# A second feed-forward product as two nested levels of seven half-size products, in two phases around the other block's first product

## The chip, the core and the metric

The kernel runs on one core of a Trainium2 chip. The metric is the device time of one execution in microseconds. The program before takes 2951.67 us (median of three runs, 2950.88 to 2952.83). All matrices are fp32 and lie in DRAM; a matmul reads its two operands from SBUF and adds into PSUM.

## The reference

One transformer layer on 2048 tokens of width 1024. The change touches the last step, the feed-forward part with squared ReLU:

```python
def sq_relu_mlp(h, w1, w2):
    return jnp.square(jax.nn.relu(h @ w1)) @ w2
...
        h2 = modulate(x, norm2_g[l], sh2, sc2)
        x = x + g2 * sq_relu_mlp(h2, w_ff1[l], w_ff2[l])
```

`w_ff1` is 1024 x 4096, `w_ff2` is 4096 x 1024. `g2` is one factor per channel (M2 in the kernel), `x` the residual (x1_d).

## The kernel before

Everything is held transposed: 128 channels on the partitions, 512 tokens (TB) along a row. The four groups of 512 tokens form two blocks of 1024.

**Precision.** TensorE multiplies fp32r operands. Each fp32 operand is split into a high half h (a cast on ScalarE, ACT) and a low half l = x - h (a subtraction on VectorE, DVE). A product of two operands is three matmuls, hh, hl and lh (`product`, lines 1971 to 1973). Each has 128 x 128 weights and 512 moving columns.

**Seven products.** A matrix product of 2 x 2 quarters is made of seven products of quarters, with sums of quarters as operands and of results behind them (the Strassen-Winograd form). The before kernel does that at one level in both feed-forward products.

**Four stages**, in this order: `ff1(0)`, `ff2(0)`, `ff1(1)`, `ff2(1)`; the number is the block.

- `ff1` (first product) runs over 16 groups of 256 hidden channels. `ff1_group` makes seven products per group, adds the results on DVE (line 1981; five of the additions read PSUM, four read SBUF alone), applies ReLU and square on ACT, and stores the seven operands that `ff2` needs: `ao_d[blk][p]`. `w1_ops` prepares the weights of the next group beside it.
- Beside `ff1(0)`, `w2_ops` reads two row tiles of `w_ff2` per group, forms four sums on DVE (lines 1957 to 1961) and stores the seven weight operands, `wo_d[p]` (printed as w2o_d).
- `ff2` (second product) runs over seven products p and 8 chunks c each, 56 steps. A step loads 512 KB of `ao_d` and 512 KB of `wo_d`, splits both (`ff2_cast`, lines 2088 and 2089), and makes 24 matmuls into four PSUM banks. The results are added up in PSUM where possible, then scaled by M2 and added to the residual on DVE (`scaled`, line 2123), and stored.
- Beside `ff2(0)`, `h_ops` and `mod_part` prepare the operands of `ff1(1)`. GpSimd (POOL) has nothing to do in any of the four stages.

**What sets the order.** Each engine works its instructions in the order of the program, and waits by semaphores. In `ff2` that order is pinned to the code's. Loads and stores are issued by SyncE (SP), in order too. Buffers come in rings by tag (POOLS): b4 and f2 hold 1024 and 512 fp32 columns, hb 512. A load waits until the oldest buffer of its ring is free.

Of the kernel before, what the change touches and what calls it, by code (L numbers as in the profile page):

```python
# [48 lines left out]
SPLIT = (2, 0)  # L49


def f32(ap):
# [48 lines left out]
class Kern:  # L101
# [127 lines left out]
    def constants(self):  # L229
# [81 lines left out]
        self.wo_d = operands("w2o")  # L311
# [1426 lines left out]
    def halves(self, raw, p=None, kk=None):  # L1738
        nc = self.nc
        tags = ("hb", "hb")  # L1740
        if p in (0, 5):
            tags = ("in", "in")
        elif p == 1 and kk < 3:
            tags = (("raw", "raw"), ("raw", "gx"), ("gx", "hb"))[kk]
        h, l = (self.sb(t, [TB], F32R) for t in tags)
        nc.scalar.copy(h, raw)
        nc.vector.tensor_tensor(out=l, in0=raw, in1=f32(h), op=ALU.subtract)
        return h, l
# [103 lines left out]
    def h_ops(self, blk, ops, mod):  # L1852
# [3 lines left out]
        xs, r, turned = [], None, 0  # L1856

        def quarters():
            for kk in range(HK):
                x = self.sb("f8", [2, 2, TB])  # L1860
                xs.append(x)
                for i in range(2):
                    for j in range(2):
                        while kk > turned + 1:
                            yield
                        self.x1_quarter(x, blk, kk, i, j)
                        yield

        loads = quarters()
        for at, _ in enumerate(mod):  # L1870
            if at >= 3:
                next(loads, None)
            if 6 <= at < 9:
                r = next(spread)
            yield
        for kk in range(HK):
            x = xs[kk]
            self.x1_scaled(x, r)
            next(loads, None)
            yield  # L1880
            raw = self.x1_turned(x, kk)
            turned += 1
            yield
            next(loads, None)
# [6 lines left out]
            next(loads, None)  # L1891
# [4 lines left out]
            next(loads, None)  # L1896
# [48 lines left out]
    def w2_ops(self, s):  # L1945
        nc = self.nc
        tt, sub = nc.vector.tensor_tensor, ALU.subtract
        rows = self.I["w_ff2"][0]
        r = self.sb("f9", [2, 2, TB])
        nc.sync.dma_start(  # L1950
            r.rearrange("p j n c -> p j (n c)"),
            rows[2 * s * P : (2 * s + 2) * P].rearrange("(j p) c -> p j c", p=P),
        )
        yield
        b11, b12, b21, b22 = r[:, 0, 0], r[:, 0, 1], r[:, 1, 0], r[:, 1, 1]
        t1, t2, t3, t4 = (self.sb("f2", [TB]) for _ in range(4))
        tt(out=t1, in0=b12, in1=b11, op=sub)
        tt(out=t2, in0=b22, in1=t1, op=sub)
        yield
        tt(out=t3, in0=b22, in1=b12, op=sub)  # L1960
        tt(out=t4, in0=b21, in1=t2, op=sub)
        yield
        for p, src in enumerate((b11, b21, b22, t4, t1, t2, t3)):
            nc.sync.dma_start(self.wo_d[p][s // 2][s % 2], src)
        yield
# [77 lines left out]
    def ff1(self, blk, h, extra, w=None, late=()):  # L2043
        if w is None:
            w = {0: {}}
            for _ in self.w1_ops(0, w[0]):
                pass
        late = iter(late)
        for g in range(NG):
            nxt = iter(())  # L2050
            if g + 1 < NG:
                w[g + 1] = {}
                nxt = self.w1_ops(g + 1, w[g + 1])
            else:
                raws = [self.ff2_load(blk, 0, c) for c in range(2)]
                self.ready = [self.ff2_cast(raws.pop(0))], raws
            more = extra(g)
            for _ in self.ff1_group(blk, g, w.pop(g), h):
                next(late, None)
                next(nxt, None)  # L2060
                next(more, None)
            for _ in nxt:
                pass
            for _ in more:
                pass

    def ff2_load(self, blk, p, c, apart=False):
        raw = []
        for src in (self.ao_d[blk][p][c], self.wo_d[p][c]):
            if apart:  # L2070
                ls = [self.sb("hb", [TB], F32R) for _ in range(2)]
                for s, l in enumerate(ls):
                    self.nc.sync.dma_start(f32(l), src[s])
            else:
                ls = self.sb("b4", [2, TB], F32R)
                self.nc.sync.dma_start(f32(ls), src.rearrange("s p c -> p s c"))
            raw.append(ls)
        return raw

    def ff2_cast(self, raw):  # L2080
        nc = self.nc
        out = []
        for ls in raw:
            apart = isinstance(ls, list)
            pairs = []
            for l in ls if apart else [ls]:
                h = self.sb("hb", [TB], F32R) if apart else self.sb("b4", [2, TB], F32R)
                nc.scalar.copy(h, f32(l))  # L2088
                nc.vector.tensor_tensor(out=l, in0=f32(l), in1=f32(h), op=ALU.subtract)  # L2089
                pairs += [(h, l)] if apart else [(h[:, s], l[:, s]) for s in range(2)]  # L2090
            out.append(pairs)
        return out

    def ff2(self, blk, side):
        nc = self.nc
        add, mult = ALU.add, ALU.mult
        order = (0, 1, 5, 6, 4, 2, 3)
        steps = [(p, c) for p in order for c in range(NCH)]
        ahead = 4 if blk else 3

        def load(n):
            return self.ff2_load(blk, *steps[n], blk and n > 2 and n % 2)

        begin = self.here()
        ready, raws = self.ready
        raws += [load(n) for n in range(2, ahead)]
        stores = []
        goes = {1: (0, 0), 4: (1, 1), 2: (0, 1), 3: (1, 0)}
        u2, u3, xs = ([None] * TT for _ in range(3))

        def place(p, t):
            i, j = goes[p]
            return 2 * blk + i, j * TT + t

        def residual(p):
            for t in range(TT):
                b, k = place(p, t)
                xs[t] = self.sb("f2", [TB])
                nc.sync.dma_start(xs[t], self.x1_d[b][k * P : (k + 1) * P, :])

        def scaled(p, t, out, src):
            _, k = place(p, t)
            nc.vector.scalar_tensor_tensor(  # L2123
                out=out, in0=src, scalar=self.M2[:, k : k + 1], in1=xs[t], op0=mult, op1=add
            )

        def carried(p, ts):
            for t in ts:
                scaled(p, t, xs[t], (u3 if p == 4 else u2)[t])

        def leave(p, t, src):
            b, k = place(p, t)
            c = self.sb("f2", [TB])
            scaled(p, t, c, src)

            def store(queue=nc.sync):
                queue.dma_start(
                    self.out[k * P : (k + 1) * P, b * TB : (b + 1) * TB], c
                )

# [48 lines left out]
        for _ in side:  # L2189
            pass  # L2190
# [459 lines left out]
```

## Time and profile before

| | us |
|---|---|
| median of three runs | 2951.67 |
| the profiled execution | 2947.45 |
| its span on the core | 2945.7 |
| `ff1(0)`, from 1698.8 | 315.6 |
| `ff2(0)`, from 2014.4 | 311.1 |
| `ff1(1)`, from 2325.5 | 309.9 |
| `ff2(1)`, from 2635.4 | 306.2 |

The stages are bounded by where the operands of the matmuls change in the trace. The profile has one line of tenths per engine, in 40 slices of the span (a 9 is busy for 90% or more). Its groups of instructions give engine, operation, out<-in by tile name, shape and count, then busy us and the mean ns of one. PE is TensorE's matmuls, PEld its weight loads.

### The profile page before, as it was taken

How to read it: one execution, taken by the hardware profiler on the slowest of the kernel's cores; microseconds unless marked ns; L12 is line 12 of the kernel's file. 1: busy time of each engine (PE TensorE's matmuls, PEld its weight loads, DVE VectorE, ACT ScalarE, POOL GpSimd, SP SyncE). 2: the span in 40 equal slices, each digit the busy share in tenths (PEclk: the TensorE clock that was granted, in tenths of full speed). 3: DMA queues.
4: the chain of work that ended last, by engine and by line, in shares of the span. 5: the costliest groups of instructions: out<-in, count | busy, mean ns of one | idle time of the engine just before them, and what ended most of it. 6: DMA issues, size and time to landing. Idle time of an engine off the chain costs nothing.

```text
span 2945.7 us, 39124 instructions
## 1 busy us (share of the span) xinstructions
PE 2880.6 (98%) x14062; PEld 2177.6 (74%) x14062; DVE 2037.2 (69%) x2946; ACT 1393.3 (47%) x1997; POOL 674.3 (23%) x472
## 2 busy tenths in 40 slices
PE   8999999999999999999999999999999999999999
PEld 7877788777555555447888878888888888888887
DVE  6857387875888988877555797876676666654554
ACT  6545765552455554554222354444463444444442
POOL 0000000000999999983333200000000000000000
PEclk9999999999999999999999999999999999999999
DMA  8688867786110100117666578888766543456663
GB/s 312 192 297 275 300 214 232 251 268 223 51 34 30 37 31 26 34 58 248 203 212 197 170 264 300 310 288 302 255 237 232 172 148 140 148 185 247 229 219 143
DMA packets 387955, 568.04 MB, mean 193 GB/s; under 512 B 41952, under 2 KB 180880, under 8 KB 387760
## 3 DMA queue, kind: packets, MB, share of 16 engines
q1 hardware_dynamic: 375456, 544.83, 55.2%
q10 hardware_dynamic: 12304, 20.71, 1.9%
q8 instruction: 110, 1.80, 0.3%
q14 instruction: 85, 0.70, 0.1%
HBM read 382.78 MB, written 182.58 MB: 192 GB/s over the span
## 4 chain that ended last, share of the span: by engine, by line
PE 73%; DVE 3%; DMA 2%; ACT 1%; issue 1%; SPq 0%; POOL 0%; DVEq 0%; ACTq 0%; POOLq 0%
PE b L1971 13%; PE b L1973 13%; PE b L1972 13%; PE o L2534 8%; PE s L2520 7%; PE b L215 4%; PE b L217 4%; PE b L216 4%; PE m L2463 3%; DVE ts L2473 1%; DMA gm_d<-t 1%; PE m L2576 0%; PE a L1971 0%; PE a L1973 0%; PE a L1972 0%
## 5 line engine op out<-in xcount | busy, mean ns | idle before, releaser
L2473 DVE TENSOR_REDUCE ts<-m 128x1 f32<-128x512 f32 x472 | 300.1, 681 | 52.5 <-PE m L2463 50.1
L2089 DVE TENSOR_TENSOR b<-b,b 128x1024 fp32r<-128x1024 f32 x170 | 200.8, 1221 | 145.5 <-ACT b L2088 145.1
L2554 POOL TENSOR_TENSOR ac<-ac,p 128x512 f32<-128x512 f32 x160 | 269.8, 1708 | 38.1 <-ACT p L2526 37.7
L2088 ACT CAST b<-b 128x1024 fp32r<-128x1024 f32 x170 | 170.6, 1051 | 213.2 <-PE b L1972 95.7
L1973 PE MATMUL b<-b,b 128*128 128x512 f32 x680 | 265.5, 390 | 1.3 <-DVE b L2089 1.2
L1971 PE MATMUL b<-b,b 128*128 128x512 f32 x680 | 265.8, 391 | 0.2 <-DVE f L2123 0.2
L1972 PE MATMUL b<-b,b 128*128 128x512 f32 x680 | 265.0, 390 | 0.0
L2526 ACT ACTIVATE p<-s 128x1024 f32<-128x1024 f32 x149 | 152.2, 1025 | 218.1 <-PE s L2520 197.0
L2554 POOL TENSOR_TENSOR ac<-ac,t 128x512 f32<-128x512 f32 x184 | 249.2, 1381 | 4.5 <-ACT t L2526 4.5
L2520 PE MATMUL s<-h,h 64*128 64x512 f32 x1728 | 228.2, 392 | 0.0
L2520 PEld LDWEIGHTS s<-h,h 64*128 64x128 f32 x1728 | 161.5, 185 | 39.7 <-ACT t L2526 3.6
L1972 PE MATMUL b<-hb,b 128*128 128x512 f32 x446 | 174.3, 391 | 0.0
L1981 DVE TENSOR_TENSOR f<-f,b 128x512 f32<-128x512 f32 x160 | 109.4, 684 | 88.7 <-issue 48.6
L1973 PE MATMUL b<-hb,b 128*128 128x512 f32 x415 | 161.7, 390 | 0.0
L1971 PE MATMUL b<-hb,b 128*128 128x512 f32 x415 | 161.7, 390 | 0.0
L2534 PE MATMUL o<-p,h 128*64 128x512 f32 x596 | 159.5, 617 | 0.0
L1973 PEld LDWEIGHTS b<-b,b 128*128 128x128 f32 x680 | 127.7, 188 | 29.4 <-DVE b L2089 3.0
L1971 PEld LDWEIGHTS b<-b,b 128*128 128x128 f32 x680 | 127.7, 188 | 27.0 <-issue 0.8
L1972 PEld LDWEIGHTS b<-b,b 128*128 128x128 f32 x680 | 127.8, 188 | 26.9 <-issue 0.2
L2463 PEld LDWEIGHTS m<-h,h 64*128 64x128 f32 x584 | 60.6, 184 | 114.9 <-DVE ts L2473 94.2
L2534 PE MATMUL o<-t,h 128*64 128x512 f32 x556 | 142.9, 592 | 0.0
L2526 ACT ACTIVATE t<-s 128x1024 f32<-128x1024 f32 x139 | 141.5, 1018 | 0.0
(486 smaller groups left out, 7055.0 us busy)
## 6 DMA issues: line engine op xcount, KB each, us to landing
ao_d<-f SPq DMA_DIRECT2D x224, 256.0 KB
f<-in_w_ff SPq DMA_DIRECT2D x48, 1024.0 KB
b<-ao_d SPq DMA_DIRECT2D x85, 512.0 KB
b<-w2o_d SPq DMA_DIRECT2D x85, 512.0 KB
w2o_d<-f SPq DMA_DIRECT2D x112, 256.0 KB
f<-in_w_in SPq DMA_DIRECT2D x38, 512.0 KB
f<-x_d SPq DMA_DIRECT2D x64, 256.0 KB
hb<-ao_d SPq DMA_DIRECT2D x54, 256.0 KB
```

The source lines that it names most:

```text
L215: mm(ps, sh, mh, start=start, stop=False)
L1971: mm(ps, wh, hh, start=start and k == 0, stop=False, skip_group_check=True)
L1972: mm(ps, wh, hl, start=False, stop=False, skip_group_check=True)
L1973: mm(ps, wl, hh, start=False, stop=k == len(w) - 1, skip_group_check=True)
L2088: nc.scalar.copy(h, f32(l))
L2089: nc.vector.tensor_tensor(out=l, in0=f32(l), in1=f32(h), op=ALU.subtract)
L2463: nc.tensor.matmul(out, self.q[0][rows, tok], key[rows], start=True, stop=True)
L2473: nc.vector.tensor_reduce(out=self.mx[:, t, h, c : c + 1], in_=ps[h], axis=AX.X, op=ALU.max)
L2520: nc.tensor.matmul(s[:, h], w[rows], x[rows], start=j < PAIR and n == 0, stop=n == len(terms) - 1, skip_group_check=True,)
L2526: nc.scalar.activation(pt, s, AF.Exp)
L2534: nc.tensor.matmul(self.o[h * HD : (h + 1) * HD, :], k.V[c][:, i, self.kv * HD : (self.kv + 1) * HD], pt[:, h], start=j == 0, stop=j == NK ...
L2554: nc.gpsimd.tensor_tensor(out=self.acc[e][:, h], in0=old[:, h], in1=pt[:, h], op=ALU.add)
```

## The change

The second product of both blocks becomes one product of 2048 x 4096 by 4096 x 1024, made of seven outer products (tokens by block, hidden channels by halves, output channels by halves), each of which is made of seven inner products (the level that was there). 49 products of 48 matmuls each take the place of 14 of 192.

- **Two phases.** Outer products 0 and 1 need only block 0's operands. They run as `ff2_first` between `ff1(0)` and `ff1(1)`: 56 steps of 12 matmuls. The other five run as `ff2_second` after `ff1(1)`: 7 inner products q of 20 steps (`steps`). What the first phase leaves for the second goes through DRAM (`us_d`).
- **Weights.** `w_ff2` is laid out anew on the host (w2a, w2b). A side chain makes the operands: `w2_first` (8 rounds, in `ff1(0)`), then `mod_part`, then `w2_second` (16 rounds, the rest of `ff1(0)` and `ff1(1)`). Their sums are on GpSimd. They store `wa_d` and `wb_d`, in pieces of 1 KB and 512 B a row.
- **Token operands.** Phase two loads the four quarters of an inner operand (`quarter`) and forms the four outer sums s1 to s4 from them (`outer_sum`): s2 on DVE, s1, s3 and s4 on GpSimd, but for three of the first s1, on DVE.
- **Splits.** One step has a token split (1024 columns), every second step a weight split (1024 columns), which serves two steps. The weight split's subtraction is on GpSimd in phase one, on DVE in phase two.
- **Results.** `prepare` and `finish` add the inner results; `prepare`'s additions are on GpSimd.
- `h_ops` no longer runs `mod_part`; `w1_ops(0)` of block 1 moves into phase one.

The core of the diff (`where` and `residual` are address helpers):

```diff
-    "back": {"f8": 2, "f2": 16, "fs": 5},
-    "rest": {"hb": 35, "b4": 12, "f9": 1},
+    "back": {"f8": 2, "f2": 17, "fs": 5},
+    "rest": {"hb": 18, "b4": 13},
...
+    def inner_sums(self, views):
+        tt, sub = self.nc.gpsimd.tensor_tensor, ALU.subtract
+        for b11, b12, b21, b22 in views:
+            tt(out=b11, in0=b12, in1=b11, op=sub)
+            tt(out=b12, in0=b22, in1=b12, op=sub)
+        yield
+        for b11, b12, b21, b22 in views:
+            tt(out=b22, in0=b22, in1=b11, op=sub)
+            tt(out=b21, in0=b21, in1=b22, op=sub)
...
+    def w2_second(self):
+        nc = self.nc
+        dma, tt, sub = nc.sync.dma_start, nc.gpsimd.tensor_tensor, ALU.subtract
+        for k in range(KQ):
+            for ch in range(2):
...
+                tt(out=rb[:, 0], in0=ra[:, 0], in1=rb[:, 0], op=sub)
+                tt(out=ra[:, 0], in0=ra[:, 1], in1=ra[:, 0], op=sub)
+                yield
+                tt(out=rc, in0=ra[:, 1], in1=rb[:, 0], op=sub)
+                tt(out=rb[:, 1], in0=rb[:, 1], in1=rc, op=sub)
...
+                for r, slot in tiles:
+                    dma(dst[4, slot], r[:, 0])
+                    dma(dst[5:7, slot].rearrange("q p c -> p q c"), r[:, 2:])
+                pairs = [[r[:, :, a] for a in range(4)] for r in (ra, rb)]
+                yield from self.inner_sums(pairs + [[rc[:, a] for a in range(4)]])
...
+                for r, slot in tiles:
+                    dma(dst[:4, slot].rearrange("q p c -> p q c"), r)
...
+    def a_cast(self, t, apart=False):
+        h = self.sb("b4", [2, TB], F32R)
+        l = self.sb("b4", [2, TB], F32R) if apart else t
+        self.nc.scalar.copy(h, f32(t))
+        self.nc.vector.tensor_tensor(out=l, in0=f32(t), in1=f32(h), op=ALU.subtract)
...
+    def w_cast(self, t, eng):
+        h = self.sb("b4", [4, 2, P], F32R)
+        self.nc.scalar.copy(h, f32(t))
+        eng.tensor_tensor(out=t, in0=f32(t), in1=f32(h), op=ALU.subtract)
...
+    def prepare(self, q, key, ch, base=None):
+        pool = self.nc.gpsimd.tensor_tensor
...
+                pool(out=t, in0=v, in1=base, op=ALU.add)
+            self.sized(q, key, ch, self.xs[at], t)
...
+    def first_cast(self, n):
+        if n < len(self.steps):
+            self.ac[n] = self.a_cast(self.ar.pop(n))
+            if n % 2 == 0:
+                self.wc[n] = self.w_cast(self.wr.pop(n), self.nc.gpsimd)
...
+    def outer_sum(self, qi, name, kp, eng):
+        A = self.A[qi]
+        if name == "s1":
...
+            out, x, y, op = A["s1", kp // 2][:, kp % 2], A["21", kp], A["22", kp], ALU.add
+        elif name == "s3":
+            out, x, y, op = A["21", kp], A["11", kp], A["21", kp], ALU.subtract
+        elif name == "s2":
+            x = A["s1", kp // 2][:, kp % 2]
+            out, y, op = A["11", kp], A["11", kp], ALU.subtract
+        else:
+            out, x, y, op = A["12", kp], A["12", kp], A["11", kp], ALU.subtract
+        eng.tensor_tensor(out=f32(out), in0=f32(x), in1=f32(y), op=op)
...
+        seq = [(4, 0), (4, 1)] + [(5, k) for k in range(4)] + [(4, 2), (4, 3)]
+        seq += [(o, k) for o in (6, 3, 2) for k in range(4)]
+        self.steps = [(qi, o, kp) for qi in range(7) for o, kp in seq]
...
+    def second_cast(self, n):
+        if n < len(self.steps):
+            qi, o, kp = self.steps[n]
+            self.ac[n] = self.a_cast(self.outer_operand(qi, o, kp), o != 3)
+            if n % 2 == 0:
+                self.wc[n] = self.w_cast(self.wr.pop(n), self.nc.vector)
...
+        for kp, s in enumerate((4, 8, 10, 12)):
+            later.setdefault(s, []).append(("s1", kp, pool))
+        for kp in range(4):
+            later.setdefault(14 + kp, []).extend([("s3", kp, pool), ("s2", kp, dve)])
+            later.setdefault(18 + kp, []).append(("s4", kp, pool))
...
+        side = chain()
+        self.ff1(0, h, side, self.open_first, w, late)
+        h, w = self.operand_lists(), {0: {}}
+        self.ff2_first(self.h_ops(1, h), self.w1_ops(0, w[0]))
+        self.ff1(1, h, side, self.open_second, w)
...
+        self.ff2_second()
```

Where it moves instructions, in the orders of the two programs (line, operation, out<-in by tile, shape). DVE in the last stage before, `ff2(1)`, inside one product; b4 and hb are the operands being split, and only their casts' results go in beside them:

```order
L2089 TENSOR_TENSOR b4_4579_24987<-b4_4579_24987,b4_4605_25129 128x1024
L2089 TENSOR_TENSOR b4_4580_24989<-b4_4580_24989,b4_4606_25132 128x1024
L2089 TENSOR_TENSOR hb_4585_25029<-hb_4585_25029,hb_4609_25163 128x512
L2089 TENSOR_TENSOR hb_4586_25030<-hb_4586_25030,hb_4610_25166 128x512
L2089 TENSOR_TENSOR hb_4587_25033<-hb_4587_25033,hb_4611_25169 128x512
L2089 TENSOR_TENSOR hb_4588_25034<-hb_4588_25034,hb_4612_25172 128x512
```

DVE in `ff2_second`, in the last steps of the third inner product (L2115 splits tokens, L2126 weights, L2287 is an outer sum into a quarter's buffer hb, L2195 an addition that reads the PSUM bank b):

```order
L2287 TENSOR_TENSOR hb_4465_24206<-f8_4436_24058,hb_4465_24206 128x1024
L2115 TENSOR_TENSOR b4_4480_24282<-hb_4392_23844,b4_4479_24281 128x1024
L2126 TENSOR_TENSOR b4_4470_24230<-b4_4470_24230,b4_4481_24285 128x1024
L2287 TENSOR_TENSOR hb_4469_24227<-f8_4436_24058,hb_4469_24227 128x1024
L2115 TENSOR_TENSOR b4_4484_24305<-hb_4397_23868,b4_4483_24304 128x1024
L2195 TENSOR_TENSOR in_4297_23390<-in_4297_23390,b_4423_23982 128x512
L2195 TENSOR_TENSOR in_4298_23398<-in_4298_23398,b_4424_23983 128x512
L2287 TENSOR_TENSOR hb_4473_24252<-f8_4461_24184,hb_4473_24252 128x1024
L2115 TENSOR_TENSOR b4_4488_24329<-hb_4402_23895,b4_4487_24328 128x1024
L2126 TENSOR_TENSOR b4_4476_24275<-b4_4476_24275,b4_4489_24332 128x1024
```

And GpSimd at the same place (L2287 are s1 into f8, s3 and s4; L2162 adds results):

```order
L2287 TENSOR_TENSOR f8_4461_24184<-hb_4457_24164,hb_4460_24182 128x1024
L2162 TENSOR_TENSOR in_4285_23331<-in_4285_23331,f2_4467_24217 128x512
L2162 TENSOR_TENSOR in_4286_23333<-in_4286_23333,f2_4468_24225 128x512
L2287 TENSOR_TENSOR hb_4416_23967<-hb_4465_24206,hb_4416_23967 128x1024
L2287 TENSOR_TENSOR hb_4432_24038<-hb_4469_24227,hb_4432_24038 128x1024
L2287 TENSOR_TENSOR hb_4441_24081<-hb_4473_24252,hb_4441_24081 128x1024
L2287 TENSOR_TENSOR hb_4457_24164<-hb_4475_24271,hb_4457_24164 128x1024
L2162 TENSOR_TENSOR in_4314_23480<-in_4314_23480,f2_4444_24093 128x512
L2162 TENSOR_TENSOR in_4315_23488<-in_4315_23488,f2_4445_24101 128x512
L2287 TENSOR_TENSOR hb_4482_24300<-hb_4482_24300,hb_4465_24206 128x1024
```

Splits of 512 columns are gone, sums stand between the splits on DVE, and GpSimd, which had no row after the merge of the branches, has such rows throughout. DVE's sum into hb_4465 overwrites what GpSimd's sum into hb_4416 reads.

The weight sums of `ff1`: on DVE before, in `ff1(0)`, between the additions of the group,

```order
L1957 TENSOR_TENSOR f2_3225_16787<-f9_3221_16767 128x512
L1958 TENSOR_TENSOR f2_3226_16788<-f9_3221_16767,f2_3225_16787 128x512
L1960 TENSOR_TENSOR f2_3227_16789<-f9_3221_16767 128x512
L1961 TENSOR_TENSOR f2_3228_16790<-f9_3221_16767,f2_3226_16788 128x512
L1981 TENSOR_TENSOR f2_3219_16763<-f2_3219_16763,b_3218_16750 128x512
```

and on GpSimd now, the first eight rows of a round of `w2_second` (the inner sums of two more tiles follow):

```order
L1991 TENSOR_TENSOR b4_3414_18112<-b4_3413_18111,b4_3414_18112 128x512
L1992 TENSOR_TENSOR b4_3413_18111<-b4_3413_18111 128x512
L1994 TENSOR_TENSOR f2_3415_18113<-b4_3413_18111,b4_3414_18112 128x512
L1995 TENSOR_TENSOR b4_3414_18112<-b4_3414_18112,f2_3415_18113 128x512
L1949 TENSOR_TENSOR b4_3413_18111<-b4_3413_18111 128x2x128
L1950 TENSOR_TENSOR b4_3413_18111<-b4_3413_18111 128x2x128
L1953 TENSOR_TENSOR b4_3413_18111<-b4_3413_18111 128x2x128
L1954 TENSOR_TENSOR b4_3413_18111<-b4_3413_18111 128x2x128
```

The four rows per group leave DVE; 16 rows per round stand on GpSimd.

More of the change, by code (lines that the diff above doesn't have):

```diff
@@ L2041, in ff1_group, with ff1 @@
         yield
[L2043 to L2047, printed above, removed]
+    def ff1(self, blk, h, side, opened, w, late=()):
         late = iter(late)
@@ L2060, in ff1 @@
                 next(nxt, None)
-                next(more, None)
+                if 1 - blk <= g < NG - 1:
+                    next(side, None)
             for _ in nxt:
                 pass
[L2064 to L2073, printed above, removed]
-            else:
[L2075 to L2092, printed above, removed]
@@ new lines, in ff1, with a_load @@
+            if blk == 0 and g == 2:
+                self.norms(NB - 1)
+    def a_load(self, q, blk, half, kp, tag="b4"):
+        t = self.sb(tag, [2, TB], F32R)
+        src = self.ao_d[blk][q][half * (NCH // 2) + kp]
+        self.nc.sync.dma_start(f32(t), src.rearrange("s p c -> p s c"))
+        return t
+    def a_cast(self, t, apart=False):
[3 more added lines that the diff above has]
+        self.nc.vector.tensor_tensor(out=l, in0=f32(t), in1=f32(h), op=ALU.subtract)
+        return [(h[:, s], l[:, s]) for s in range(2)]
@@ new lines, in finish @@
+    def finish(self, q, key, ch, ps, base=None):
+        nc = self.nc
+        add = partial(nc.vector.tensor_tensor, op=ALU.add)
+        at = key, ch
+        tag = "in" if any(key) else "f2"
+        if q == 0:
+            v = self.V2[at] = self.sb(tag, [TB])
+            if base is None:
+                nc.scalar.copy(v, ps)
+            else:
+                add(out=v, in0=base, in1=ps)
+            return
+        if q == 6:
+            if base is None:
+                self.V3[at] = self.sb(tag, [TB])
+            v = self.V3[at]
+            add(out=v, in0=v if base is not None else self.V2[at], in1=ps)
+            return
+        if q in PLACE:
+            b, k = self.where(q, key, ch)
+            c = self.sb("f2", [TB])
+            self.sized(q, key, ch, c, ps)
+            dst = self.out[k * P : (k + 1) * P, b * TB : (b + 1) * TB]
+            if q == INNER[-1] and key == (0, 1):
+                (nc.scalar if ch else nc.sync).dma_start(dst, c)
+            else:
+                self.stores.append((dst, c))
+        if q in (4, 5):
+            add(out=self.V2[at], in0=self.V2[at], in1=ps)
@@ new lines, in ff2_first @@
+    def ff2_first(self, side, w1):
+        begin = self.here()
+        banks, key = {}, (0, 0)
+        for n, (q, o, kp) in enumerate(self.steps):
+            self.first_a(n + 4)
+            if n % 2 == 0:
+                self.first_w(n + 4)
+            self.flush()
+            self.first_cast(n + 2)
+            if n and n % 2 == 0:
+                next(side, None)
+            if n >= len(self.steps) - 7:
+                next(w1, None)
+            if (o, kp) == (0, 0):
+                banks[q] = [self.bank([TB]) for _ in range(2)]
+            if o and q in PLACE and kp in (0, 2):
+                for ch in range(2):
+                    if kp:
+                        self.prepare(q, key, ch)
+                    else:
+                        self.residual(q, key, ch)
+            a, w = self.ac.pop(n), self.wc[n - n % 2]
+            for ch, ps in enumerate(banks[q]):
+                self.product(ps, self.w_tiles(w, kp, ch), a, (o, kp) == (0, 0))
+                if kp < NCH // 2 - 1:
+                    continue
+                if o:
+                    self.finish(q, key, ch, ps)
+                else:
+                    u = self.sb("f2", [TB])
+                    self.nc.scalar.copy(u, ps)
+                    self.stores.append((self.us_d[q][ch], u))
+        self.flush()
```

394 lines of the change are left out of this document (251 added, 143 removed).

## Prediction

> **What bounds the kernel now.** I read the page first, then the four feed-forward stages as windows, then the groups of instructions inside them, then the places where VectorE and GpSimd work at the same time.
>
> ```profile
> span 2945.7 us, 39124 instructions
> PE 2880.6 (98%) x14062; PEld 2177.6 (74%) x14062; DVE 2037.2 (69%) x2946; ACT 1393.3 (47%) x1997; POOL 674.3 (23%) x472
> ...
> PE   8999999999999999999999999999999999999999
> ...
> DVE  6857387875888988877555797876676666654554
> ...
> POOL 0000000000999999983333200000000000000000
> ...
> GB/s 312 192 297 275 300 214 232 251 268 223 51 34 30 37 31 26 34 58 248 203 212 197 170 264 300 310 288 302 255 237 232 172 148 140 148 185 247 229 219 143
> ```
>
> TensorE is never idle for long, so fewer matmuls are worth their time one for one, as long as the other engines keep up. And GpSimd (POOL) does nothing in the last 17 of the 40 slices, which is where the change works. The same by stage (first product of block 0, second of block 0, first of block 1, second of block 1; the bounds are where the moving operands of the matmuls change):
>
> ```profile
> core 0: us, PE busy (x) PEld busy (x) DVE busy (x) ACT busy (x) POOL busy (x), PEclk, DMA share, GB/s
> 1698.80:2014.40 315.60, 313.15 (x1344) 253.36 (x1345) 246.00 (x337) 152.14 (x225) 0.00 (x0) 0.99 0.82 291
> 2014.40:2325.50 311.10, 310.25 (x1374) 255.58 (x1373) 204.93 (x226) 151.87 (x179) 0.00 (x0) 1.00 0.72 245
> 2325.50:2635.40 309.90, 309.90 (x1346) 252.58 (x1345) 192.04 (x249) 140.07 (x203) 0.00 (x0) 1.00 0.43 148
> 2635.40:2941.60 306.20, 305.44 (x1345) 252.07 (x1343) 150.37 (x193) 122.72 (x182) 0.00 (x0) 1.00 0.61 216
> ```
>
> Each stage is 1344 matmuls (the 1374 holds some 30 small others) and is TensorE from end to end: 306.2 / 1345 = 0.2277 us for a matmul. VectorE (DVE) has 70 to 156 us of slack in each.
>
> **What one operation costs.** Groups of the same stretch; behind the first bar stand busy us and the mean ns of one, behind the second the idle time before them:
>
> ```profile
> L2089 DVE TENSOR_TENSOR b<-b,b 128x1024 fp32r<-128x1024 f32 x170 | 200.8, 1221 | 145.5 <-ACT b L2088 145.1
> L2088 ACT CAST b<-b 128x1024 fp32r<-128x1024 f32 x170 | 170.6, 1051 | 213.2 <-PE b L1972 95.7 <-PE b L1973 89.4 <-issue 14.1
> L1981 DVE TENSOR_TENSOR f<-f,b 128x512 f32<-128x512 f32 x160 | 109.4, 684 | 88.7 <-issue 48.6 <-PE b L1973 39.9
> L1747 DVE TENSOR_TENSOR hb<-f,hb 128x512 fp32r<-128x512 f32 x34 | 23.0, 687 | 3.1 <-ACT hb L1746 2.7
> L2123 DVE SCALAR_TENSOR_TENSOR f<-f,M,f 128x512 f32<-128x512 f32 x16 | 11.3, 745 | 0.0
> L1957 DVE TENSOR_TENSOR f<-f 128x512 f32<-128x512 f32 x16 | 11.0, 686 | 0.0
> L1794 DVE TENSOR_TENSOR f<-f,g 128x2048 f32<-128x2048 f32 x4 | 9.1, 2285 | 0.0
> ```
>
> A split of 1024 columns is an ACT cast (1.05 us) and a DVE subtraction (1.22 us, both inputs in SBUF). 512 columns take 0.685 us, so the fixed part of a DVE operation is 2 x 0.685 - 1.221 = 0.15 us.
>
> The change puts much work on GpSimd beside such subtractions. Nothing in the feed-forward part shows the two together, but the attention does, where GpSimd adds 512 columns (L2554) while VectorE adds 1024 (L2551, both inputs in SBUF) or reads matmul results (L1666). First minimum, median and maximum of these lines, then the timelines of both engines at one place:
>
> ```profile
> L2551 DVE TENSOR_TENSOR ac<-ac,p x36: 1207/1220/2347, 752.7 to 1326.8; 128x1024 f32<-128x1024 f32 x36
> L2554 POOL TENSOR_TENSOR ac<-ac,t x184: 1257/1276/2278, 737.0 to 1310.1; 128x512 f32<-128x512 f32 x184
> L1666 DVE SCALAR_TENSOR_TENSOR gt<-gt,b x62: 616/687/689, 1344.4 to 1648.3; 128x512 f32<-128x512 f32 x62
> ```
> ```profile
> 1101.25 2.34 DVE L2551 TENSOR_TENSOR ac<-ac,p 128x1024 f32<-128x1024 f32 x1
> ```
> ```profile
> 1101.22 3.50 POOL L2554 TENSOR_TENSOR ac<-ac,p 128x512 f32<-128x512 f32 x2
> ```
>
> GpSimd's first addition starts at 1101.22 and needs its 1.26. VectorE starts 0.03 later, is held until then, and ends at 1103.59. GpSimd's second addition is held meanwhile, and ends at 1104.72. So the two take turns: two GpSimd additions of 1.26 and one of VectorE took 3.50 us together, and VectorE's part of that is 3.50 - 2.51 = 0.99 us of its 1.22. The operation that reads a matmul result is never stretched (689 at most, while GpSimd is busy). I call 0.99 us for 1024 columns (half for 512) VectorE's **turn**. A turn of GpSimd is 1.26 us for 512 columns. For 1024 no row exists: between 1.26 (all of it fixed) and 2.52 (none). I take 2.37, with the same fixed part as VectorE's, 2 x 1.26 - 0.15.
>
> The Trainium skill's page "SBUF — State Buffer", section "Who interferes with whom", has this as a rule that speaks against the change: a VectorE instruction with two SBUF inputs and a GpSimd instruction that reads SBUF exclude each other for the whole instruction. The trace agrees but for the fixed part: 3.50 us where whole instructions make 2.51 + 1.22 = 3.73. By whole instructions the second phase would be the upper end worked out for it below, 551 us, and not 478.
>
> **The change, stage by stage** (counts from the code and from the order of both programs).
>
> *Matmuls.* 49 small products of 48 matmuls, 2352, in place of 2688: 336 fewer, 336 x 0.2277 = 76.5 us. The two phases have 14 x 48 = 672 (153 us) and 35 x 48 = 1680 (382.5 us). The two stages of the first product keep their 1344.
>
> *First product, block 0.* The weight sums leave VectorE (64 x 0.685 = 44 us of 246) and go to GpSimd in pieces: 8 rounds of eight 256-column operations, and five rounds of the second kind (four of 512, eight of 256, four of 128). With the fixed part of 0.15, a 256 is 0.70 and a 128 is 0.43: 8 x 5.6 + 5 x 12.3 = 106 us. Even if VectorE waits for all of them, 246 - 44 + 106 = 308 us, under the stage's 315.6. **No change**, 0 to +10.
>
> *First phase (was 311.1).* Three limits. TensorE: 153 us. Turns: 56 token splits x 0.99, four scalings of 2048 (8), 54 operations of 512 at 0.5 for the other block's operands and residuals, the next stage's first weights (5), and on GpSimd 28 weight splits x 2.37: 55 + 8 + 27 + 5 + 66 = 161 us. DMA: 84 loads of 0.52 MB, 46 transfers of 0.26 MB and 1 MB of weights, 57 MB; the highest slice of the page moved 312 GB/s, which gives 183 us, and 291 GB/s at a share of 0.82 would be 355 at full share, 161 us. I take **172 us**, -139; between 160 and 190.
>
> *First product, block 1 (309.9).* The other eleven rounds, 11 x 12.3 = 135 us of GpSimd beside 192 of VectorE. If all of it held VectorE up, 327, 17 us too much; but nearly a third of VectorE's work reads matmul results (five L1981 a group, 80 x 0.684 = 55 us) and isn't held. **+4**, 0 to +17. SP gets 15 stores a round behind GpSimd's sums; it waits there for GpSimd, and the next group's weights are queued behind it, which is what the upper end is for.
>
> *Second phase (was 306.2).* VectorE has 140 token and 70 weight splits and 31 sums of 1024 columns, 24 residuals of 512 with both inputs in SBUF, and about 33 us that read matmul results. GpSimd has 81 sums of 1024 and 28 additions of 512. VectorE alone: 241 x 1.22 + 24 x 0.75 + 33 = 345 us, 90% of TensorE's 382.5; it would just fit. But the turns add up: 241 x 0.99 + 12 + 81 x 2.37 + 28 x 1.26 = 239 + 12 + 192 + 35 = **478 us**. The last of the seven products has no sums ahead of it (turns 43 us, TensorE 55), so 478 - 43 + 55 = 490. Taking turns without a gap is the best case: GpSimd's sums of a product bunch in its last six steps, and VectorE can be only two steps ahead of TensorE. I take **500 us**, +194. The ends: 464, if GpSimd's 1024 cost 2.2 (81 x 0.17 = 14 less), and 551, if nothing of an operation hides beside the other engine's (241 x 1.22 + 24 x 0.75 + 81 x 2.52 + 28 x 1.26).
>
> *Sum.* 315.6 + 172 + 314 + 500 = 1301.6 against 1242.8: +59. The profiled execution took 2947.45 us, so 3006; the median of the runs is 4.2 above it, so **3010**. The end of the program stays one scaling and one store behind the last matmul.
>
> **The rivals.**
>
> *Turns cost little* (faster): GpSimd's sums fall into VectorE's gaps, or are short beside what the attention shows. Then TensorE bounds: phases 165 and 388, 2951.7 - 146 + 82 + 2 = 2890. For it: VectorE alone fits. Against: the pair shown took turns, L2551 reaches 2347 ns and L2554 2278, and in the second phase the turns are 478 us in 382. It decides if both engines' turns stay below 382 us.
>
> *A long GpSimd sum costs hardly more than a short one* (faster): at 1.26 for 1024, turns are 239 + 12 + 102 + 35 = 388, so 405 for the stage; the first phase stays with DMA, 169. 2951.7 - 142 + 99 + 3 = 2912. VectorE's own rows speak against it (1.22 against 0.685), and no GpSimd row for it.
>
> The Trainium skill's page "GPSIMD Engine Reference", section "Elementwise — side-by-side cycle accounting", states 4497 ns for an addition of 2048 columns; with the 1.26 of the rows that makes an estimated 2.34 for 1024, and 476 us of turns. No run here shows it.
>
> *VectorE waits for GpSimd's sums themselves* (slower still): in the steps 14 to 17 of each product VectorE's sum overwrites what GpSimd's sum of the same quarter reads, so VectorE, which works in order, stands until that is done, and the next splits stand behind it. At 2.4 us each, 4 x 6 x 2.4 = 58 us more: 3068. It decides when GpSimd comes to these sums late, which it does if it is the busier one.
>
> **How the numbers follow.** Forecast (turns bound the second phase): 0.70. Its low ends together give 2951.7 + (160 - 311.1) + (464 - 306.2) = 2958, its high ends (190, 551, +27) 3102. Waits on top, about 3068: 0.11, within that range. Turns cost little: 0.12. Cheap long sums: 0.07. The predicted time is the first's, 3010. The range runs from 2955 to 3100 and leaves the two faster cases out. About 0.2% (6 us) is what a measurement of this kernel can tell from no change: faster 0.18, the same 0.03, slower 0.79.
>
> **What would show it.** In the second phase: subtractions of 1024 columns with a mean well above 1.22 us (near 2), TensorE idle by a fifth or more with VectorE's subtraction as its releaser, VectorE nearly full, and a stage of about 500 us. In the first phase, about 172 us with a DMA share near 0.9. In the first product's stages, nothing or little. Wrong would be: the mean stays at 1.22 beside a busy GpSimd, or TensorE stays full in the second phase (then 2890), or the idle time is behind loads and not behind VectorE.

## The result, and the profile after

| | us |
|---|---|
| before, median of four runs | 2951.28 (2946.62 to 2952.83) |
| after, median of four runs | 3198.01 (3189.83 to 3204.83) |
| ratio, 95% interval | 1.0838 (1.0809 to 1.0867) |
| the profiled execution after; its span | 3196.33; 3194.5 |

The change makes the kernel 8.4% slower. The forecast was 3010 with a range up to 3100: the sign was right, the size was far too small, and the time lies outside the range.

The page of after, the lines that answer to those of before (engines' totals, then tenths in 40 slices, with the granted clock as PEclk):

```profile
span 3194.5 us, 39874 instructions
PE 2915.9 (91%) x13726; PEld 2154.2 (67%) x13726; DVE 2358.4 (74%) x2945; ACT 1469.1 (46%) x2041; POOL 1380.0 (43%) x929
...
PE   8999999999999999999999979888888996888788
...
DVE  6765588758888888665568656588765666999997
...
POOL 0000000007999998633332325433455544556652
PEclk9999999999999999999999989999999998999889
```

TensorE is no longer full in most slices from the 24th on, and the 24th lies in `ff1(0)`. VectorE (DVE) is full in slices 35 to 39 only, all in the second phase, so a full VectorE there does not explain the holes before it. The four stages of after as windows (`ff1(0)`, first phase, `ff1(1)`, second phase; the columns are those of the same table of before):

```profile
1691.80:2075.50 383.70, 336.64 (x1371) 265.74 (x1370) 241.27 (x297) 152.56 (x227) 144.79 (x146) 0.93 0.72 238
2075.50:2286.70 211.20, 176.64 (x687) 131.67 (x686) 171.56 (x149) 121.10 (x150) 69.22 (x27) 0.96 0.77 268
2286.70:2646.20 359.50, 323.53 (x1336) 256.71 (x1336) 225.56 (x249) 137.69 (x203) 195.43 (x177) 0.96 0.71 227
2646.20:3190.40 544.20, 437.17 (x1681) 337.27 (x1679) 484.17 (x313) 231.48 (x254) 294.11 (x108) 0.89 0.59 203
```

| stage | before | after | difference | forecast | missed |
|---|---|---|---|---|---|
| `ff1(0)`, to the start of the next | to 2014.4 | to 2075.5 | +61 | 0 | 61 |
| first phase | 311.1 | 211.2 | -100 | -139 | 39 |
| `ff1(1)` | 309.9 | 359.5 | +50 | +4 | 46 |
| second phase | 306.2 | 544.2 | +238 | +194 | 44 |

The differences make the 249 us between the two spans. (The first matmul of `ff1(0)` came 7.0 us earlier after the change, so the first row compares where it ends.) The miss of 190 us is spread over all four stages, and over half of it lies in the two where the forecast had nothing or little.

### The profile page after: what moved, and what is told of

It reads as the page before. It is cut to its first block, busy times and chain, and to the rows that moved or that the text cites. A ratio compares the mean times of both kernels' runs of the same rounds, so it can differ in the third digit from the quotient of the medians.

```text
span 3194.5 us, 39874 instructions
## 1 busy us (share of the span) xinstructions
PE 2915.9 (91%) x13726; PEld 2154.2 (67%) x13726; DVE 2358.4 (74%) x2945; ACT 1469.1 (46%) x2041; POOL 1380.0 (43%) x929
## 5 line engine op out<-in xcount | busy, mean ns | idle before, releaser
L2016 PE MATMUL b<-b,b 128*128 128x512 f32 x784 | 327.9, 418 | 32.3 <-DVE b L2126 26.6
L2014 PE MATMUL b<-b,b 128*128 128x512 f32 x784 | 324.9, 414 | 25.2 <-ACT b L2114 17.7
L2015 PE MATMUL b<-b,b 128*128 128x512 f32 x676 | 282.8, 418 | 61.7 <-DVE b L2115 58.9
L2015 PE MATMUL b<-hb,b 128*128 128x512 f32 x554 | 224.5, 405 | 19.2 <-DVE hb L2115 19.2
L2016 PEld LDWEIGHTS b<-b,b 128*128 128x128 f32 x784 | 157.8, 201 | 80.5 <-DVE b L2126 38.2
L2015 PEld LDWEIGHTS b<-b,b 128*128 128x128 f32 x676 | 136.2, 201 | 108.9 <-DVE b L2115 79.8
L2014 PEld LDWEIGHTS b<-b,b 128*128 128x128 f32 x784 | 157.7, 201 | 64.5 <-ACT b L2114 23.1
L2287 POOL TENSOR_TENSOR hb<-hb,hb 128x1024 f32<-128x1024 f32 x55 | 173.1, 3165 | 58.3 <-DVE f L2287 16.8
L2014 PE MATMUL b<-hb,b 128*128 128x512 f32 x415 | 167.3, 404 | 13.5 <-DVE f L2024 13.1
L2024 DVE TENSOR_TENSOR f<-f,b 128x512 f32<-128x512 f32 x160 | 109.1, 682 | 91.8 <-PE b L2016 86.6
L2016 PE MATMUL b<-hb,b 128*128 128x512 f32 x415 | 163.8, 396 | 0.0
L2125 ACT CAST b<-b 128x1024 fp32r<-128x1024 f32 x98 | 102.8, 1049 | 103.1 <-PE b L2015 99.8
L2114 ACT CAST b<-hb 128x1024 fp32r<-128x1024 f32 x110 | 113.2, 1049 | 80.4 <-PE b L2016 57.4
L2027 ACT ACTIVATE f<-f 128x512 f32<-128x512 f32 x96 | 60.6, 631 | 188.7 <-DVE f L2024 185.3
```

Of the source, the lines that this page charges most:

```text
L2014: mm(ps, wh, hh, start=start and k == 0, stop=False, skip_group_check=True)
L2015: mm(ps, wh, hl, start=False, stop=False, skip_group_check=True)
L2016: mm(ps, wl, hh, start=False, stop=k == len(w) - 1, skip_group_check=True)
L2024: nc.vector.tensor_tensor(out=out, in0=in0, in1=in1, op=op)
L2114: self.nc.scalar.copy(h, f32(t))
L2125: self.nc.scalar.copy(h, f32(t))
```

## What the second phase shows

Groups of the second phase of after (engine, operation, out<-in, count; busy us and mean ns of one; the idle time before them and what ended it):

```profile
L2287 POOL TENSOR_TENSOR hb<-hb,hb 128x1024 f32<-128x1024 f32 x55 | 173.1, 3165 | 58.3 <-DVE f L2287 16.8 <-DVE hb L2287 16.8 <-DMA hb<-ao_d 14.4
L2126 DVE TENSOR_TENSOR b<-b,b 128x1024 fp32r<-128x1024 f32 x69 | 128.4, 1861 | 6.1 <-ACT b L2125 6.1
L2145 DVE SCALAR_TENSOR_TENSOR f<-f,M,f 128x512 f32<-128x512 f32 x16 | 32.4, 2061 | 0.0
L2145 DVE SCALAR_TENSOR_TENSOR f<-b,M,f 128x512 f32<-128x512 f32 x23 | 16.6, 737 | 2.3 <-PE b L2016 2.3
```

The weight split takes 1.86 us instead of 1.22. The same line L2145 takes 2.06 us where both its large inputs are in SBUF (`f<-f,M,f`) and 0.74 where one of them is a matmul result (`f<-b,M,f`). How the turns look, first VectorE and then GpSimd (POOL), each row with its start and duration:

```profile
2867.92 3.43 DVE L2126 TENSOR_TENSOR b<-b,b 128x1024 fp32r<-128x1024 f32 x1
2871.27 3.41 DVE L2115 TENSOR_TENSOR hb<-hb,b 128x1024 fp32r<-128x1024 f32 x1
2874.61 0.68 DVE L2195 TENSOR_TENSOR in<-in,b 128x512 f32<-128x512 f32 x1
```
```profile
2866.87 10.07 POOL L2287 TENSOR_TENSOR hb<-hb,hb 128x1024 f32<-128x1024 f32 x3
```

One subtraction and one sum of 1024 columns together take 3.35 us (2867.92 to 2871.27), then 3.34. The forecast's turns were 2.37 + 0.99 = 3.36. So the price of a turn was right.

What TensorE waits for in this phase, in which it is idle for 107 us (total us, times, longest):

```profile
PE b L2015 <- DVE b L2115: 34.9, 22, 4.5
PE b L2016 <- DVE b L2126: 26.6, 26, 2.8
PE b L2015 <- DVE hb L2115: 19.2, 8, 6.0
...
PE b L2015 <- DMA b<-wb_d: 1.5, 1, 1.5
```

VectorE's subtractions make 81 of the 107 us, as forecast, and loads hardly anything. VectorE itself is idle for 60 us of the phase. The waits for ScalarE's casts make 40 of them, and the first and the last of the seven inner products hold about 33 (the windows' columns as above):

```profile
DVE b L2115 <- ACT b L2114: 19.5, 10, 6.3
DVE hb L2115 <- ACT b L2114: 14.7, 7, 3.8
DVE b L2126 <- ACT b L2125: 6.1, 6, 1.3
```
```profile
2650.00:2738.00 88.00, 54.76 (x187) 39.65 (x188) 68.44 (x36) 31.95 (x36) 52.09 (x17) 0.81 0.65 234
3121.00:3191.00 70.00, 64.25 (x263) 50.82 (x263) 56.31 (x50) 30.16 (x33) 12.92 (x6) 0.95 0.35 121
```

## The experiments

All are edits of the kernel after. T (turns) is the forecast's mechanism. Q and Q2 say that SP stands behind GpSimd's sums in the side chain's stores, so that the next group's weights come late; T1 that GpSimd's short weight sums hold VectorE in `ff1` too; R that the ring of 1024-column tiles stays taken until the sums are done; D that transfers in small pieces are slow. O, M and S are named in the expectations where they are tested. The expectations call some runs by a label: e2 has outer sums that only write, e4 leaves the weight sums out, and e3, e5 and e6 move outer sums, weight splits and weight sums to VectorE. Most expectations let the first phase end and `ff1(1)` begin at the first matmul of `ff1(1)`, which stands 17 us ahead of the phase's last one: the 194 and 377 there are the 211 and 360 of the tables here. The 368 and 369 for the two `ff1` stages, and the 540 for the second phase, come from rougher bounds (1698 to 2066, 2281 to 2650, 2650 to 3190). Single executions, if nothing else is said; the times of before beside them were 2949 to 2953 us.

### The second phase: sums that only write, and sums on VectorE

```diff
+        if eng is self.nc.gpsimd:
+            eng.memset(f32(out), 0.0)
```

> Left out: the outer sums on GpSimd in the second phase are fills of the same buffer with zero, which write SBUF and read nothing. Theory T (GpSimd's reads and VectorE's second input take turns, and the turns bound the second phase, 540 us): VectorE's subtractions of 1024 columns there go from means of 1.5-2.1 us back to 1.22, and the stage falls to 390-430, total about 3070. Rival O (the order binds it: VectorE stands behind sums that come late, and loads come late): the means of the operations fall little, the stage stays above 490.

Measured 3084.18, the second phase 435.4, 5 us above the expected stretch. GpSimd's outer sums (their values are left out) became writes of a constant. Two groups of that phase:

```profile
L2126 DVE TENSOR_TENSOR b<-b,b 128x1024 fp32r<-128x1024 f32 x69 | 86.1, 1247 | 7.6 <-ACT b L2125 7.6
L2288 POOL MEMSET hb<- 128x1024 f32 x55 | 51.6, 958 | 132.4 <-DVE f L2290 59.2 <-DMA hb<-ao_d 45.4 <-DVE hb L2290 27.9
```

VectorE's split is back at 1.25 us. The writes are also shorter than the sums (0.96 us), so this run alone does not separate holding from GpSimd's own lateness; the pairs above do, and for `ff1` a run with longer writes below.

```diff
     def outer_sum(self, qi, name, kp, eng):
+        eng = self.nc.vector if qi else eng
```

> All outer sums but those of the first inner product on VectorE (72 more sums of 1024 columns there, 72 fewer on GpSimd). Theory T: a sum costs 1.22 us on VectorE and a turn of 2.37 on GpSimd, so although VectorE is the fuller engine the stage falls, to VectorE's own 345 + 72 x 1.22 = 433 and some gaps: 445-475 us, total 3105-3140. Without turns (the fuller engine gets more work): 482 + 88 = 570 us, total about 3230.

Measured 3144.51, the second phase 496.2. More work on the fullest engine makes the phase 48 us shorter, which an exclusion of the two engines explains and the faster rivals do not. But it is longer than expected. The windows of the phase, of the run with the sums on VectorE:

```profile
2642.40:3138.60 496.20, 423.34 (x1681) 330.06 (x1679) 432.79 (x385) 231.61 (x254) 70.56 (x36) 0.92 0.64 223
```

VectorE is idle for 496.2 - 432.8 = 63 us here, and for 544.2 - 484.2 = 60 us in the kernel after. The forecast had put 22 us on top of the turns (500 - 478), 12 of them for the last inner product. So the idle time is hardly due to the turns: it stays when the sums leave GpSimd.

### The first phase: the weight splits on VectorE

```diff
-                self.wc[n] = self.w_cast(self.wr.pop(n), self.nc.gpsimd)
+                self.wc[n] = self.w_cast(self.wr.pop(n), self.nc.vector)
```

> The first phase (194 us, forecast 172) with its 28 weight splits on VectorE instead of GpSimd. By turns: VectorE alone has 56 and 28 splits at 1.22, four scalings (9), 54 operations of 512 columns (37) and 5, about 153 us, so the phase falls to DMA's 161 to 183, about 175. If loads bound it now: unchanged, 188 to 194. The other stages stay, total 3180 to 3198.

Measured 3180.20. The phase, bounded by its own matmuls, went from 211.2 to 188.8, 22 us less; in the bounds of the expectation it is 172, close to the 175 expected. The whole phase and its first half, in this run:

```profile
2077.80:2266.60 188.80, 168.88 (x690) 128.16 (x689) 156.32 (x175) 120.86 (x151) 0.00 (x0) 0.99 0.84 299
2077.80:2172.00 94.20, 85.74 (x355) 65.02 (x353) 76.31 (x90) 63.05 (x80) 0.00 (x0) 1.00 0.92 336
```

VectorE is busy for 156 of 189 us, and the transfers are at a share of 0.92 in the first half. That they are what is left there is read from this row and was not tried.

### The first product: is it SP's queue?

```diff
-        nc.sync.dma_start(
+        nc.scalar.dma_start(
             raw.rearrange("p k f c -> p (k f c)") ...
```

> The load of the next group's first weights (1 MB, w1_ops) is issued from ACT's queue instead of SP's; nothing else changes. Theory Q (in the two stages of the first product, 368 and 369 us, SP works in order and stands behind GpSimd's weight sums, so this load is issued late and TensorE waits for it): both stages fall to 315-335 us, the total from 3198 to about 3110. Rival D (the small pieces and the traffic of the DMA itself make the loads late) and rival T1 (VectorE is held up by GpSimd's small sums): both stages stay at 360 or more, total 3185-3205.

Measured 3212.20, 14 us slower: the first phase began at 2088.9, `ff1(1)` took 366.7. Taking the W1 load out of SP's queue gains nothing here, although the cast's wait for it in `ff1(0)` fell from 34.2 to 21.8 us. On ACT's queue the load stands behind ACT's own work instead, so this run alone does not rule Q out; the run that frees the stores, below, is the better test.

```diff
     def inner_sums(self, views):
+        if True:
+            yield
+            return
...
-                tt(out=rb[:, 0], in0=ra[:, 0], in1=rb[:, 0], op=sub)
-                tt(out=ra[:, 0], in0=ra[:, 1], in1=ra[:, 0], op=sub)
```

> Left out: all sums of the second product's weights on GpSimd during the first product's stages; the loads and stores stay, in number and size. Theory Q and rival T1 both expect 315-325 us for these two stages (now 368 and 369) and a total of about 3095; rival D expects 350 or more. Together with the run that moves the load: if that gains as much as this one, it is the queue; if only this one gains, it is VectorE held up by the sums.

Measured 3112.49 with all weight sums left out and the stores kept: the first phase began at 2038.4, `ff1(1)` took 308.9, as before the change. So the sums cost nearly all of `ff1(1)`'s loss, and D falls there.

```diff
-        dma = self.nc.sync.dma_start
+        dma = self.nc.gpsimd.dma_start
```

> The side chain's loads and stores are issued by GpSimd instead of SP. Q2 by SP's queue: SP no longer waits for a sum, W1 loads go out in time, ff1(1) 326 to 340, ff1(0) 346 to 355, total 3110 to 3140. R (the ring of 1024-column tiles is held until the sums and stores are done): SP still waits for a free buffer, so ff1 stays within 10 us of 384 and 377, total 3180 to 3200. T1: the same, about 3198.

Measured 3399.57, 201 us slower (the same edit stands in `w2_second`). GpSimd issues a store in 0.57 to 0.76 us of its own time, between its sums:

```profile
L2008 POOL DMA_DIRECT2D wb_d<-b x44 | 33.6, 764 | 54.8 <-issue 54.6
L2001 POOL DMA_DIRECT2D wb_d<-b x44 | 31.5, 716 | 8.9 <-issue 8.7
L2000 POOL DMA_DIRECT2D wb_d<-b x44 | 24.9, 567 | 0.0
```

`ff1(1)` grew to 489.9 us. It brings a cost of its own and tells none of the theories apart.

```diff
+            z = self.cut(b11)
+            for _ in range(2):
+                tt(out=z, in0=z, in1=z, op=sub)
-            tt(out=b11, in0=b12, in1=b11, op=sub)
-            tt(out=b12, in0=b22, in1=b12, op=sub)
```

> Where the two first-product stages lose some 60 us each (ff1(0) 384, ff1(1) 377; 346 and 326 without the weight sums, e4). Here GpSimd does as many sums of the same sizes, but on a tile of its own (the sums' results are left out of the weights, one addition of 512 columns a round excepted), so no store waits for a sum and no tile is kept for one. The ring of 512-column tiles is one buffer shorter for it. Q2 (SP stands behind the sums in the side chain's stores, and the next group's W1 load is queued behind it; or the ring of 1024-column tiles is held): as e4, ff1(0) about 346, ff1(1) about 326, total about 3115. T1 (GpSimd's sums hold VectorE by taking turns): nothing changes, 384 and 377, total about 3198.

Measured 3196.24, and it is no answer either. The sums, on a tile of their own, depended on nothing any more and were placed far earlier in GpSimd's order: in `ff1(1)` (309.9 us) GpSimd is busy for 19.6 us and not for 195, and before `ff1(0)` the sums stood ahead of other work of GpSimd, which put off the first matmuls. The next run ties them to the load.

### The first product: held by reads

```diff
-            tt(out=b11, in0=b12, in1=b11, op=sub)
-            tt(out=b12, in0=b22, in1=b12, op=sub)
+            tt(out=self.cut(b11), in0=b12, in1=b11, op=sub)
+            tt(out=self.cut(b12), in0=b22, in1=b12, op=sub)
```

> GpSimd's weight sums read the loaded tiles as before but write to a spare tile of their own (left out of the weights, all but one addition of 512 a round), so the side chain's stores on SP wait for the load and not for the sums, while the tile stays taken until the sums have read it, and the sums have two SBUF inputs as before. The ring of 512-column tiles is one shorter for it. Q2 (SP standing behind sums delays the W1 loads): ff1(1) falls from 377 to 327 to 335, ff1(0) from 384 to 346 to 352, total about 3110 to 3125. T1 (VectorE held by turns): 370 to 384 each, total about 3190. R (the ring): the same as T1, or a little less as the sums start earlier.

```diff
+    def written(self, out, **_):
+        for _ in range(3):
+            self.nc.gpsimd.memset(out, 0.5)
```

> Each weight sum on GpSimd is replaced by three writes of a constant to the same place (the sums are left out): about the same time on GpSimd (a write of 1024 columns took 0.96 us in e2, of 512 0.53), with every wait on it as before, but no input from SBUF; in e2 VectorE's subtractions stayed at 1.22 to 1.28 us beside such writes. T1: VectorE is free, so ff1(0) and ff1(1) go to about 346 and 326, total about 3115. Q2 and R: SP and the tiles wait as long as before, so 370 to 384 each, total about 3190.

Measured 3178.30 with sums that only read the tiles, and 3120.36 with writes in their place. `ff1(1)` of after was 359.5, 50 more than before: TensorE was idle for 36 us of it and 14 us longer busy (323.5 against 309.9). The windows of it, first the reads, then the writes:

```profile
2270.00:2625.60 355.60, 327.21 (x1336) 260.62 (x1335) 243.62 (x249) 138.86 (x203) 196.59 (x177) 0.95 0.72 230
```
```profile
2247.70:2567.90 320.20, 312.63 (x1335) 252.03 (x1335) 192.17 (x249) 138.18 (x203) 158.40 (x529) 0.99 0.80 255
```

GpSimd is busy for 197 and 158 us of them. With the stores freed from the sums, 4 us are gained; with the stores still behind GpSimd and its reads taken away, 39. VectorE's busy time is 243.6 beside reads and 192.2 beside writes; before the change it was 192.0. The additions of `ff1_group` (L2024 of after) show where it goes: first those with both inputs in SBUF and those that read PSUM in `ff1(1)` of after, then the first kind beside the writes (L2028 there):

```profile
L2024 DVE TENSOR_TENSOR f<-f,f 128x512 f32<-128x512 f32 x61 | 50.7, 851 | 18.8 <-ACT f L2028 16.9 <-POOL f L1949 1.4
L2024 DVE TENSOR_TENSOR f<-f,b 128x512 f32<-128x512 f32 x79 | 53.8, 681 | 38.1 <-PE b L2016 35.6 <-DMA wb_d<-b 2.0 <-issue 0.3
```
```profile
L2028 DVE TENSOR_TENSOR f<-f,f 128x512 f32<-128x512 f32 x61 | 40.7, 687 | 11.9 <-ACT f L2032 11.3
```

Only the first kind is stretched. So T1 holds in `ff1`, and Q2 is worth 4 us in this stage. In `ff1(0)` the start of the first phase moved by 12 us with the stores freed and by 32 with the writes. R was not tried by itself: with writes the tiles are kept as long as GpSimd works on them, and nearly all of the time is gone all the same. Late W1 loads are not it either: the cast of those weights waits 29.8 us for them beside the writes, and 34.6 in after.

The Trainium skill's page "SBUF — State Buffer", section "Who interferes with whom", says that a VectorE instruction with two SBUF inputs contends with a GpSimd instruction that reads SBUF, and not with one that only writes it. The two windows agree.

```diff
-        tt, sub = self.nc.gpsimd.tensor_tensor, ALU.subtract
+        tt, sub = self.nc.vector.tensor_tensor, ALU.subtract
```

> All weight sums of the side chain on VectorE. VectorE gets 63 us in ff1(0) and 80 in ff1(1) (7.2 us a round at 0.685 for 512, 0.42 for 256, 0.28 for 128 columns, estimates from its rows), 265 and 272 of 310 to 316. T1: no turns any more, so ff1(0) about 346, ff1(1) about 326, total about 3115. Q2: a sum is done in a third of the time but stands in VectorE's order behind the splits, so half of it at most: 365 and 350, total about 3150.

Measured 3116.60: the first phase begins at 2039.4 (36 us earlier), `ff1(1)` takes 318.3 (41 less). Its window:

```profile
2246.70:2565.00 318.30, 311.52 (x1336) 251.13 (x1335) 254.17 (x425) 138.17 (x203) 2.40 (x1) 0.99 0.80 257
```

VectorE is busy for 254 us here and for 226 in the slower stage of after. So its load was never the limit. What changes, as read from the waits, is how late one operation can be. In `ff1(1)` of after, ScalarE's ReLU (L2027) and its copy of a product's result (L2035), and TensorE behind the copy:

```profile
ACT f L2027 <- DVE f L2024: 87.4, 38, 4.9
...
PE b L2014 <- ACT f L2035: 28.0, 12, 6.8
```

and with the sums on VectorE:

```profile
ACT f L2027 <- DVE f L2024: 72.0, 36, 5.5
...
PE b L2014 <- ACT f L2035: 2.8, 2, 2.1
```

The copy, which frees TensorE's bank, stands in ScalarE's order behind operations that wait for VectorE, and VectorE's SBUF additions of 512 columns (L2024) have the means of 0.85 us in this stage of after and 0.69 with writes that are shown above.

### What is left of ff1(0)

```diff
-            yield from self.mod_part(lambda: self.sb("f2", [TB]), ("g2",), True)
+            self.nc.vector.memset(self.M2, 0.5)
+            for _ in range(11):
+                yield
```

> The weight sums on VectorE as in e6, and the side chain's middle part, mod_part (16 loads of 256 KB with their sums, which makes the factors M2), left out of ff1(0): M2 is a constant, and the chain passes as many steps. With the sums off GpSimd the first phase still began 24 us later than before the change (2039.4 against 2015.2). M (mod_part, moved there from the first phase's place, loads 4.2 MB ahead of the W1 weights): it begins at 2015 to 2027, total 3092 to 3105. S (the stores in pieces of 1 KB and 512 B, and SP's waits for them): it stays at 2035 to 2040, total about 3115. The first phase itself stays within 3 us of 207, since mod_part had left it already.

Measured 3100.87; the first phase begins at 2018.8, where it began at 2014.4 before the change. So M holds: beside the run with only the weight sums moved (2039.4), `mod_part` costs `ff1(0)` 21 us. The first phase grew from 207.3 to 220.8, which was not expected, so only 16 of them reach the end. In the trace of after, `mod_part`'s loads and who waited:

```profile
L419 SPq DMA_DIRECT2D f<-in_w_mod x16: 382/494/940, 1865.0 to 1899.4; - x16
...
who waited for it (us, times):
  ACT b L1920: 14.6, 1
```

L1920 is the cast of the next group's W1 weights. In the run with the weight sums on VectorE, beside which the 21 us are measured, this wait for `in_w_mod` is not there. About half of the 21 us is TensorE's idle time (17.8 us in `ff1(0)` there, 8.0 without `mod_part`), and the rest its busy time (326.3 and 315.5). Two of TensorE's waits from 1825 to 1880 in that run have no counterpart without `mod_part`; the second is its own matmul (L465), which waits for its own sum (L444):

```profile
PE b L2014 <- DVE f L2024: 4.2, 1, 4.2
...
PE b L465 <- DVE f L444: 3.3, 1, 3.3
```

So the 21 us are the price of `mod_part` as a whole, with its loads, sums and matmuls. What its loads alone cost is not shown. Before the change its 16 loads were issued between 2021.3 and 2068.9, in the stage that is now the first phase.

### All three moves together

The outer sums (e3), the weight splits of the first phase (e5) and the weight sums (e6) are on VectorE in one kernel.

> All three moves at once: weight sums, weight splits of the first phase, and outer sums (of the products 2 to 7) on VectorE, nothing else changed. If the three gains add (82, 19 and 54 us by e6, e5 and e3): 3198 - 155 = 3043, stages 344, 172, 334 and 496. If one engine's load only moves the wait (VectorE fuller everywhere): 3060 to 3100. Before is 2951; for less than that the second phase would have to come to about 400.

Median 3044.43 (3039.41 to 3046.13, four runs), 1.0312 of before (1.0292 to 1.0333). The three gains add as expected, 154 us in all. It is the best version here, and still slower than before by 3%. Its second phase:

```profile
2545.40:3039.30 493.90, 419.42 (x1681) 326.59 (x1679) 433.38 (x385) 231.67 (x254) 70.57 (x36) 0.93 0.64 224
```

It misses the kernel before by 93 us. To make them up here, the phase would have to take 494 - 93 = 401, and VectorE alone is busy for 433 of it.

## Why the prediction was wrong

- **`ff1(0)`: "Even if VectorE waits for all of them, 246 - 44 + 106 = 308 us, under the stage's 315.6. No change."** This step failed. It compared the sum of VectorE's work with the length of the stage. The turns there did hold VectorE, and a held operation is late for those behind it: of the 47 us that TensorE was idle there, 14.9 were behind ScalarE's copy (L2035) and 13.3 behind VectorE's additions (L2024), though VectorE is idle for over a third of the stage. Moving the weight sums to VectorE gave back 36 of the 61 us. SP's queue may have a part in this stage: freeing the stores from the sums alone gave 12, and no run sets the two fully apart.
- **`ff1(0)`, the moved `mod_part`.** The forecast's sum has no term for it, although the text of the change says that it moved there: 21 us. Some 4 us stay open.
- **`ff1(1)`: "+4, 0 to +17."** The same step failed: 41 of the 50 us come back with the sums on VectorE. The reason named for the upper end, SP's queue behind the sums, is worth 4 us in this stage.
- **First phase: 172, measured 211.** Turns were put at 161 us and transfers at 161 to 183, each as if it ran without a gap; the phase has both. As far as the runs show, the step that failed is to let the phase be as long as its longest limit. With the weight splits on VectorE 22 us come back; 17 stay, with the transfers at a share of 0.92 in the first half as the likely cause, not tried.
- **Second phase: 500, measured 544, within its own ends 464 and 551.** The mechanism and the price of a turn were right (3.34 us a pair, forecast 3.36). The term that was mis-sized is the time in which VectorE waits on top of the turns: 22 us put down (500 - 478), 60 measured, 40 of them for ScalarE's casts. With the turns, 478 + 60 = 538.
- **The rivals.** *Turns cost little* and *a long sum costs hardly more* are out: a sum of 1024 columns took 2.34 us at the least, and the pair takes turns. *VectorE waits for GpSimd's sums themselves*, 58 us, is out as well: VectorE's sum waited 2.5 us for GpSimd's in the whole phase. An idle time of about that size is there, but two thirds of it are waits for ScalarE's casts.
- **Why the range missed.** Each stage had an upper end of its own, and the two `ff1` stages had +10 and +17 and came out at +61 and +50. Both were worked out with the same comparison of totals, so both were wrong together. The first phase passed its end too, 211 against 190; only the second phase stayed inside.

## What to carry to other kernels

Work given to an idle engine is not free for the others when it reads SBUF beside an engine with two SBUF inputs: count it in every stage where the two run together, not only in the one where their sum exceeds the time. A total below the stage's length proves nothing for engines that work in order; ask which late operation has a buffer or bank of the bound engine behind it. And a step moved to make room takes its loads, sums and matmuls along.

## What the runs showed of the hardware

- GpSimd writes beside VectorE's two-input operations do not hold them, its reads do: 192.2 and 243.6 us of VectorE for the same work. A write of 1024 columns took 0.96 us, a sum 2.34 at the least.
- Where TensorE is interrupted, its matmuls are slower too. In the second phase of after 1681 matmuls were busy for 437.17 us, 0.260 each at a granted clock of 0.89, against 0.2277 before at 1.00. That is 1681 x 0.0324 = 54 us of TensorE's time, beside 107 of idle time. With 38.5 us idle, in the run whose sums only write, the clock was 0.96. The Trainium skill's page "TensorE: Matmul & The Clock Gate", section "HAM oscillation — how this bites in real kernels", describes such a loss by gaps. The rows here go together with that, but no run changed the gaps alone, and 0.2277/0.89 is 0.256, so the clock need not be all of it.
- A DMA issued by GpSimd took 0.57 to 0.76 us of it, and SP's `in_w_mod` loads a median of 0.49.
